# Building weight sums in DRAM: transfers in threes behind a copy that reads the weights loaded two jobs ahead

## The chip, the cores and the metric

The kernel runs on one core of a Trainium2 chip. The metric is device time in microseconds (us). Below, PE is the tensor engine, ACT the scalar engine, DVE the vector engine, POOL the GpSimd engine and SP the sync engine, which only issues DMAs. POOL issues DMAs too, and on POOL every DMA of this program takes engine time for writing its descriptors. All DMAs run on the same 16 DMA engines.

## The reference

One decoder layer on 512 positions of width 1024, in float32:

```
h = rmsnorm(x);  proj = h @ w_in                       # w_in: 1024 x 9232
y_a = short_conv_branch(bg, cg, xv) @ w_a_out
y_b = gated_delta_rule(q, k, v, z, a, b) @ w_b_out
x = x + (sigmoid(ga) * y_a + sigmoid(gb) * y_b) @ w_o  # w_o: 1024 x 1024
h = rmsnorm(x)
x = x + (silu(gate) * val) @ w_down                    # gate, val = causal conv of h @ w_up; w_down: 2816 x 1024
out = rmsnorm(x)
```

## The kernel before

**Products.** Every float32 operand is split into a high part (`wh`, made by ACT) and a low part (`wl`, made by DVE as the raw block minus `wh`; lines 140 and 141), and each product is three matmuls. Some products use a Strassen form with 7 instead of 8 block products.

**Jobs.** `run_jobs` goes through one list of jobs. A job is a weight block of 1 MB and a function `use` that emits its matmuls. While job i runs on PE, block i+1 is split and block i+2 is loaded into one of two `raw` buffers; SP issues the load as soon as the buffer's last reader is through. A plain job (`col_job`) is 48 matmuls of 512 columns. A sum job (`sum_job` with a `SumBlock`) is 84 matmuls of 256 columns, seven products of twelve; its block is split into seven pairs instead of four, and DVE first forms sums of the block's quarters in place (line 161, four additions). In a sum job the third and last product share the half bank `A[:, L]` and its neighbour: after the third product ACT and DVE take it out into `u` (lines 282 and 283), and the seventh product, the last twelve matmuls, must wait for that.

**Engines are in order.** On DVE the splits of the next block stand in one row with the `u` of the job that runs. So a `wl` that waits holds back a `u` behind it.

**Sums in DRAM.** For `w_o` and `w_down` the Strassen sums of the weights are not made by DVE but by DMAs from DRAM to DRAM, some of which accumulate: `Sums.form` (line 1028) issues them on POOL's queue, 256 KB each, 8 for each of 14 row pairs, 112 in all (32 for `w_o`, then 80 for `w_down`). Their generator stands in the queue `adds`. Before the change it is stepped once every four matmuls' worth of columns (`tick`, line 94, every 2048 columns), and it yields twice after each DMA. That paces the program text only: the DMAs stand in POOL's queue in program order, and no DMA waits for PE, so POOL issues them as fast as it gets through them. `adds` is filled in `open_conv` (line 1069), that is with the first of 24 jobs: twelve for the short convolution (C_CG, C_XV, C_BG), four C_GA, four `w_a_out`, four `w_b_out`. After them come 7 jobs for `w_o`, 22 for `w_up` (gate and value in turn; the gates of groups 2 to 9 are sum jobs) and then those for `w_down`. The `w_o` and `w_down` blocks are read from the sums (`raw<-ov`, `raw<-dv`).

**Other work of POOL there.** Four tiny powers in `fin1` (line 1301, the norm before the FFN) and four in `fin2` (line 1543, the last norm).

Of the kernel before, what the change touches and what calls it, by code (L numbers as in the profile page):

```python
# [9 lines left out]
F32 = mybir.dt.float32  # L10
# [19 lines left out]
Y_F = (5, 4, 6, 3)  # L30
WARM = 3
WQ = 12
Y_M = 10


# [24 lines left out]
def layer_kernel(ctx, tc, x, norm_mix_g, w_in, w_ab, conv_a_w, gdn_conv_w, gdn_A_log, gdn_dt_bias,  # L60
# [3 lines left out]
    pe, act, dve, pool = nc.tensor, nc.scalar, nc.vector, nc.gpsimd  # L64
# [5 lines left out]
    const = ctx.enter_context(tc.tile_pool(name="const", bufs=1))  # L70
# [4 lines left out]
    def nm(s):  # L75
        cnt[0] += 1
        return f"{s}{cnt[0]}"
# [5 lines left out]
    chains, mids, backs, evacs, splits, sums_of, adds = (deque() for _ in range(7))  # L83
    nmm = [0]

    def advance(queue, n):
        while n and queue:
            queue[0].step()
            if queue[0].done:
                queue.popleft()  # L90
            else:
                n -= 1

    def tick():
        advance(backs, 1)
        advance(mids, 1)
        advance(chains, 1)
        advance(evacs, 2)
        advance(splits, 1)
        advance(sums_of, 1)  # L100
        advance(adds, 1)

    def drain(queue):
        while queue:
            advance(queue, 1)

    def mm(o, a, b, start, stop, free=False):
        pe.matmul(o, lhsT=a, rhs=b, start=start, stop=stop, skip_group_check=free)  # L108
        nmm[0] += o.shape[-1]
        if nmm[0] >= SLAB * S:  # L110
            nmm[0] -= SLAB * S
            tick()
# [12 lines left out]
    class Block:  # L125
        def __init__(self, src, quarter=(4, P)):
            self.src, self.quarter = src, quarter
            self.raw, self.ready, self.lead = None, False, 2
            self.wh, self.wl = {}, {}

        def load(self):
# [5 lines left out]
        def part(self, name, src):  # L137
            wh = self.wh[name] = wp.tile([P, *self.quarter], F32R, tag="wh", bufs=WQ, name=nm("wh"))
            wl = self.wl[name] = wp.tile([P, *self.quarter], F32R, tag="wl", bufs=WQ, name=nm("wl"))
            act.copy(out=wh, in_=src)  # L140
            dve.tensor_tensor(out=wl, in0=src, in1=wh.bitcast(F32), op=ALU.subtract)  # L141
# [42 lines left out]
    class FormBlock(Block):  # L184
        def __init__(self, runs, names, lead, place):
            super().__init__(None, (S,))
            self.runs, self.names, self.lead, self.place = runs, names, lead, place

        def load(self):
            if self.raw is not None:  # L190
# [13 lines left out]
    def run_jobs(jobs):  # L204
        jobs[1][0].load()
        for i, (block, use) in enumerate(jobs):
            Task(block.split()).finish()
            drain(splits)
            if i + 1 < len(jobs):
                splits.append(Task(jobs[i + 1][0].split()))  # L210
            for j, (later, _) in enumerate(jobs[i + 2:i + 5]):
                if later.lead >= j + 2:
                    later.load()
            use(block.wh, block.wl)


    def piece(w, j, k):
# [7 lines left out]
    def col_job(w, i, xs, consume, pre=None):  # L225
        def use(wh, wl):
            if pre:
                pre()
            x_ = xs() if callable(xs) else xs
            for j in range(GW // P):  # L230
                o = bank()
                products(o, wh, wl, j, x_)
                evacs.append(Task(consume(j, o)))
        return Block(lambda: w[i]), use
# [25 lines left out]
    def sum_job(w, i, xs, sums, consume, place, pre=None):  # L260
        def use(wh, wl):
# [9 lines left out]
            def times(o, form, b, first):  # L271
                mm3(o, [(wh[form][:, k], wl[form][:, k], b[0][:, k], b[1][:, k]) for k in range(ND // 2)],
                    first, not first)
# [50 lines left out]
    def conv(dst, src, wcol, taps):  # L324
        act.activation(out=dst, in_=src, func=AF.Copy, scale=wcol(taps - 1))  # L325
        for j in range(taps - 2, -1, -1):
            sh = taps - 1 - j
            dve.scalar_tensor_tensor(out=dst[:, sh:], in0=src[:, :S - sh], scalar=wcol(j),  # L328
                                     in1=dst[:, sh:], op0=ALU.mult, op1=ALU.add)
            yield  # L330
# [86 lines left out]
    with tc.tile_pool(name="st1", bufs=1) as st1:  # L417
# [79 lines left out]
        def round_k(q):  # L497
            wh = k_block.wh[q] = wp.tile([P, 4, P], F32R, tag="wh", bufs=WQ, name=nm("wh"))
            act.copy(out=wh, in_=k_block.raw[:, q])

        def rest_k(q):
            wl = k_block.wl[q] = wp.tile([P, 4, P], F32R, tag="wl", bufs=WQ, name=nm("wl"))
            dve.tensor_tensor(out=wl, in0=k_block.raw[:, q], in1=k_block.wh[q].bitcast(F32), op=ALU.subtract)
# [267 lines left out]
    def mid(pr, U, um, T, rest):  # L771
        for _ in range(Y_T if pr else Y_T + Y_M):
            yield
# [211 lines left out]
    jobs = []  # L985
# [29 lines left out]
    class Sums:  # L1015
# [12 lines left out]
        def form(self):  # L1028
            steps = [[(V1, W12, False), (V3, W12, False)], [(V1, W11, True), (V3, W22, True)],
                     [(V2, None, False)], [(V2, W22, True)], [(V4, None, False)], [(V4, W21, True)]]  # L1030
            for step in steps:
                for g in self.pairs:
                    for to, q, add in step:
                        src = self.q[g][:, q] if q is not None else self.at(g, V1 if to == V2 else V2)
                        kw = dict(accum_op=ALU.add) if add else {}
                        tc.keep_in_program_order(pool.dma_start(out=self.at(g, to), in_=src, **kw))  # L1036
                        yield
                        yield

# [341 lines left out]
    def ffn(m):  # L1383
        if m < NA:
            return st["aT"][0][:, m, :]
        if len(st["aT"]) == 1:
            st["aT"].append(st["up"].tile([P, NF - NA, S], F32, tag="late", name="aTb"))
        return st["aT"][1][:, m - NA, :]

    def gate_c(g):  # L1390
        def c(j, o):
            m = 2 * g + j
            t = st["cvp"].tile([P, S], F32, tag="g", bufs=4, name=nm("g"))
            yield from conv(t, o, ff_w(m), 3)
            act.activation(out=t, in_=t, func=AF.Silu)
            gates[m] = t
            yield
        return c

    def val_c(g):  # L1400
        def c(j, o):
            m = 2 * g + j
            t = st["cvp"].tile([P, S], F32, tag="v", bufs=2, name=nm("v"))
            yield from conv(t, o, ff_w(NF + m), 3)
            dve.tensor_tensor(out=ffn(m), in0=t, in1=gates.pop(m), op=ALU.mult)
            yield
        return c
# [22 lines left out]
    for g in range(NF // 2):  # L1430
        def up_job(i, c, plain, pre=None):
            if plain:
                return col_job(w_up, i, lambda: st["h2"], c, pre)
            return sum_job(w_up, i, lambda: st["h2"], hsums, c, pair_out)

        last = g == NF // 2 - 1
        gj = up_job(g, gate_c(g), g < 2 or last, (lambda: splits.append(prep_d(prep_a, 0))) if last else None)
        vj = up_job(NF // 2 + g, val_c(g), True)
        jobs += [(gj[0], first_gate), (vj[0], first_val)] if g == 0 else [gj, vj]


# [13 lines left out]
    def prep_d(prep, c):  # L1455
        return Task(prep(ffn_pairs(down_w.pairs[2 * c], 2), xs(), 2 * c % 4))
# [107 lines left out]
    down.append((down_w.low(), use_l))  # L1564
    jobs += [(FormBlock(*what, 2 if i < 2 else min(4, i), down_place(i)), use) for i, (what, use) in enumerate(down)]
    run_jobs(jobs)
    drain(chains)

# [51 lines left out]
```

## Time and profile before

| | us |
|---|---|
| median of three runs | 971.42 (970.35 to 973.03) |
| the profiled execution | 968.61 |
| its span, first to last instruction | 966.90 |
| PE busy in the span | 954.4 |
| DVE busy | 743.9 |
| ACT busy | 506.3 |
| POOL busy | 137.1 |

The profile is of one execution. Busy time of POOL holds the writing of descriptors for its DMAs. A row of the timeline is start in us, length in us, engine, line, what it writes and reads, how many were merged, and in brackets the idle time before and what ended it. PE's matmuls overlap, so their rate is read from the distance of their starts: those of 256 columns start every 0.12 us. "SPq" is a DMA issued by SP; the time to landing is from issue until the data are there.

### The profile page before, as it was taken

To read this page: it belongs to the slowest core of one execution; us is meant where nothing else is said; L and a number is where in the kernel's file an instruction comes from. 1 tells how busy PE (TensorE), PEld (TensorE's weight loads), DVE (VectorE), ACT (ScalarE), POOL (GpSimd) and SP (SyncE) were. 2 spreads that over 40 slices of the span, in tenths; PEclk is the share of its full clock that TensorE was granted. 3 is DMA by queue.
4 is the path that set the end of the run, shared out by engine and by line. 5 is a ranking of instruction groups with operands and counts; after the bars stand their busy time and mean duration, and the time that the engine had idled before them with its cause. 6 is when DMAs were issued, how large, how long until landed. Compare 5 with 4: busy or idle time off the path is not lost. (4 is left out here: it accounts for less than half of the span.)

```text
span 966.9 us, 16043 instructions
## 1 busy us (share of the span) xinstructions
PE 954.4 (99%) x6166; PEld 826.9 (86%) x6166; DVE 743.9 (77%) x1397; ACT 506.3 (52%) x1071; POOL 137.1 (14%) x213
## 2 busy tenths in 40 slices
PE   8999999999999999999999999999999999999996
PEld 6888887987878889899988888998889999888885
DVE  6868686896635968799773479999988888969785
ACT  7795556575444434344651235645645455546463
POOL 3330300202002334234320000100000000000000
PEclk9999999999999999999999999999999999999999
DMA  6443312222222989999995235432232323177342
GB/s 226 156 138 115 100 53 88 74 75 75 55 86 76 226 228 252 252 200 260 275 260 150 87 107 220 164 119 88 88 131 87 129 90 132 44 253 235 99 132 87
DMA packets 51628, 138.10 MB, mean 143 GB/s; under 512 B 21691, under 2 KB 22112, under 8 KB 42848
## 3 DMA queue, kind: packets, MB, share of 16 engines
q1 hardware_dynamic: 39008, 107.72, 32.5%
q0 software_dynamic: 12544, 29.37, 14.8%
q8 instruction: 48, 0.79, 0.3%
q14 instruction: 28, 0.23, 0.1%
HBM read 133.64 MB, written 32.78 MB: 172 GB/s over the span
## 5 line engine op out<-in xcount | busy, mean ns | idle before, releaser
L108 PE MATMUL ps<-hT,wh 128*128 128x512 f32 (+1 forms) x1104 | 318.6, 368 | 1.2 <-DVE u L283 0.8
L140 ACT CAST wh<-raw 128x512 fp32r<-128x512 f32 x350 | 203.6, 618 | 214.3 <-PE ps L108 141.0
L141 DVE TENSOR_TENSOR wl<-raw,wh 128x512 fp32r<-128x512 f32 x350 | 232.3, 688 | 62.4 <-ACT wh L140 60.2
L108 PEld LDWEIGHTS ps<-hT,wh 128*128 128x128 f32 x1104 | 196.9, 189 | 30.1 <-DVE u L283 1.0
L108 PE MATMUL ps<-hT,wl 128*128 128x512 f32 (+1 forms) x552 | 195.2, 362 | 0.0
L108 PE MATMUL ps<-h,wh 128*128 128x512 f32 (+1 forms) x704 | 177.9, 341 | 0.3 <-DVE h L1317 0.3
L108 PEld LDWEIGHTS ps<-h,wh 128*128 128x128 f32 x704 | 122.4, 189 | 15.5 <-DVE h L1317 0.5
L108 PEld LDWEIGHTS ps<-hT,wl 128*128 128x128 f32 x552 | 104.4, 189 | 13.8
L108 PE MATMUL ps<-h,wl 128*128 128x512 f32 (+1 forms) x352 | 114.7, 341 | 0.0
L108 PE MATMUL ps<-wh,xs 128*128 128x512 f32 x312 | 96.2, 389 | 0.0
L108 PEld LDWEIGHTS ps<-h,wl 128*128 128x128 f32 x352 | 66.7, 190 | 7.6
L108 PEld LDWEIGHTS ps<-wh,xs 128*128 128x128 f32 x312 | 58.6, 188 | 12.1
L108 PE MATMUL ps<-wl,xs 128*128 128x512 f32 x156 | 60.7, 389 | 0.0
L108 PE MATMUL ps<-ts,wh 128*128 128x256 f32 x320 | 59.2, 283 | 0.0
L328 DVE SCALAR_TENSOR_TENSOR cv<-ps,wA,cv 128x511 f32<-128x511 f32 (+2 forms) x72 | 53.2, 741 | 4.0 <-ACT cv L325 3.8
L140 ACT CAST wh<-raws 128x512 fp32r<-128x512 f32 x66 | 39.2, 619 | 26.2 <-PE ps L108 12.1
L141 DVE TENSOR_TENSOR wl<-raws,wh 128x512 fp32r<-128x512 f32 x66 | 42.8, 685 | 12.1 <-ACT wh L140 12.1
L108 PEld LDWEIGHTS ps<-ts,wh 128*128 128x128 f32 x320 | 50.6, 192 | 0.0
L1543 POOL TENSOR_TENSOR r<-r,nhalf 128x1 f32<-128x1 f32 x4 | 2.2, 540 | 338.2 <-PE ps L108 331.2
L161 DVE TENSOR_TENSOR raw<-raw 128x512 f32<-128x512 f32 x72 | 49.4, 686 | 0.9
L108 PE MATMUL ps<-us,wh 128*128 128x256 f32 x256 | 47.4, 283 | 0.0
L1036 POOL DMA_DIRECT2D dv<-in_w_down_dram x50 | 35.4, 712 | 58.9 <-issue 58.4
(309 smaller groups left out, 1549.8 us busy)
## 6 DMA issues: line engine op xcount, KB each, us to landing
raw<-in_w_in_dram SPq DMA_DIRECT2D x35, 1024.0 KB, 5.5
raw<-in_w_up_dram SPq DMA_DIRECT2D x22, 1024.0 KB, 4.9
dv<-in_w_down_dram POOLq DMA_DIRECT2D x50, 256.0 KB, 7.8
raws<-dv SPq DMA_DIRECT2D x8, 768.0 KB, 7.0
ov<-in_w_o_dram POOLq DMA_DIRECT2D x20, 256.0 KB, 7.1
raws<-in_w_down_dram SPq DMA_DIRECT2D x10, 512.0 KB, 5.1
raw<-in_w_a_out_dram SPq DMA_DIRECT2D x4, 1024.0 KB, 7.7
raw<-in_w_b_out_dram SPq DMA_DIRECT2D x4, 1024.0 KB, 8.5
```

The source lines that it names most:

```text
L108: pe.matmul(o, lhsT=a, rhs=b, start=start, stop=stop, skip_group_check=free)
L140: act.copy(out=wh, in_=src)
L141: dve.tensor_tensor(out=wl, in0=src, in1=wh.bitcast(F32), op=ALU.subtract)
L161: dve.tensor_tensor(out=r[q], in0=a, in1=b, op=op)
L328: dve.scalar_tensor_tensor(out=dst[:, sh:], in0=src[:, :S - sh], scalar=wcol(j), in1=dst[:, sh:], op0=ALU.mult, op1=ALU.add)
L1036: tc.keep_in_program_order(pool.dma_start(out=self.at(g, to), in_=src, **kw))
L1543: pool.tensor_tensor(out=r, in0=r, in1=nhalf[:, 0:1], op=ALU.pow)
```

## The change

The step of `adds` is taken out of `tick`, and the second `yield` out of `form`. In its place `run_jobs` calls `feed` once for a job whose block of two jobs later is an ordinary 1 MB block (`fed`), as long as there are DMAs left: POOL copies one element of that block's raw buffer, out of its second quarter, into a tile `gate`, and then three DMAs are put out. Blocks read from the sums themselves (`FormBlock`) and the two blocks of the first `w_up` group are not `fed`. Line numbers after the change are 9 or 10 higher (1036 becomes 1046, 1301 becomes 1310).

```
 def tick():
     ...
     advance(sums_of, 1)
-    advance(adds, 1)
 ...
 class Block:
-            self.raw, self.ready, self.lead = None, False, 2
+            self.raw, self.ready, self.lead, self.fed = None, False, 2, True
 ...                                   # FormBlock: fed = False
 def run_jobs(jobs):
             ...
+            if adds and i + 2 < len(jobs) and jobs[i + 2][0].fed:
+                feed(jobs[i + 2][0].raw)
             use(block.wh, block.wl)
+
+    gate = const.tile([1, 1], F32, name="gate")
+
+    def feed(raw):
+        el = raw[0:1, 1].rearrange("p k n -> p (k n)") if len(raw.shape) == 4 else raw[0:1, 1]
+        tc.keep_in_program_order(pool.tensor_copy(out=gate, in_=el[:, 0:1]))
+        advance(adds, FEED)                                   # FEED = 3
 ...
     def form(self):                   # of Sums
                     tc.keep_in_program_order(pool.dma_start(out=self.at(g, to), in_=src, **kw))
                     yield
-                    yield
 ...
+        gj[0].fed = vj[0].fed = g > 0  # the w_up jobs of group g
```

The order of instructions on PE, ACT, DVE and SP is the same as before. On POOL it changes from the place where the sums begin. Before, behind the last power of the delta rule (`fac`), `ov` being the sums of `w_o`:

```order
L911 TENSOR_TENSOR fac_3791<-fac_3791,nhalf 128x8
L1036 DMA ov_388<-in_w_o_dram 128x512 x2
L1036 DMA ov_389<-in_w_o_dram 128x512 x2
L1036 DMA ov_390<-in_w_o_dram 128x512 x2
L1036 DMA ov_391<-in_w_o_dram 128x512 x2
```

and after, where `gate` is the new tile and each `raw` is the buffer of another block of `w_in`:

```order
L921 TENSOR_TENSOR fac_3792<-fac_3792,nhalf 128x8
L223 COPY gate<-raw_3990 1x1
L1046 DMA ov_389<-in_w_o_dram 128x512 x2
L1046 DMA ov_390<-in_w_o_dram 128x512
L223 COPY gate<-raw_4076 1x1
L1046 DMA ov_390<-in_w_o_dram 128x512
L1046 DMA ov_391<-in_w_o_dram 128x512 x2
```

Before, nothing stood between the transfers; now a copy that can only run once a load has landed stands ahead of every three. At the norm before the FFN, before, the last transfers of `w_down` (`dl`) stood ahead of the powers of `fin1`:

```order
L1036 DMA df_386<-in_w_down_dram 128x512
L1036 DMA dl<-in_w_down_dram 128x512 x4
L1301 TENSOR_TENSOR r_6694<-r_6694,nhalf 128x1
L1301 TENSOR_TENSOR r_6721<-r_6721,nhalf 128x1
L1301 TENSOR_TENSOR r_6822<-r_6822,nhalf 128x1
L1301 TENSOR_TENSOR r_6857<-r_6857,nhalf 128x1
```

and after, 63 transfers stand ahead of them and 49, behind 17 copies, follow in the FFN's first half (`raw_6836` is the first gate block of `w_up` that is fed):

```order
L1046 DMA dv_377<-in_w_down_dram 128x512
L1310 TENSOR_TENSOR r_6667<-r_6667,nhalf 128x1
L1310 TENSOR_TENSOR r_6694<-r_6694,nhalf 128x1
L1310 TENSOR_TENSOR r_6795<-r_6795,nhalf 128x1
L1310 TENSOR_TENSOR r_6830<-r_6830,nhalf 128x1
L223 COPY gate<-raw_6836 1x1
L1046 DMA dv_377<-in_w_down_dram 128x512
L1046 DMA dv_378<-in_w_down_dram 128x512 x2
```

So 49 of the 112 transfers have moved from ahead of the norm to behind it. On DVE the order stays, but in 17 of the 18 sum blocks that are fed (all but the first; nine ahead of the norm, eight in `w_up`) the first addition in place now also waits for POOL, which reads the same buffer in its copy. One such block in `w_up` before, with what each row waits for:

```order
L141 TENSOR_TENSOR wl_8570<-raw_8430,wh_8569 128x512 [waits Activation_49]
L1405 TENSOR_TENSOR aTa<-v_8442,g_8357 128x512 [waits DVE_49]
L161 TENSOR_TENSOR raw_8430<-raw_8430 128x512 [waits DVE_49]
L283 TENSOR_TENSOR u_8436<-ps_8432,u_8436 128x256 [waits Activation_49]
L161 TENSOR_TENSOR raw_8430<-raw_8430 128x512 [waits DVE_49] x2
```

and after:

```order
L141 TENSOR_TENSOR wl_8607<-raw_8459,wh_8606 128x512 [waits Activation_49]
L1414 TENSOR_TENSOR aTa<-v_8475,g_8386 128x512 [waits DVE_49]
L161 TENSOR_TENSOR raw_8459<-raw_8459 128x512 [waits DVE_49,Pool_49]
L293 TENSOR_TENSOR u_8469<-ps_8465,u_8469 128x256 [waits Activation_49]
L161 TENSOR_TENSOR raw_8459<-raw_8459 128x512 [waits DVE_49] x2
```

No row has moved; the wait for POOL stands directly ahead of the `u` that PE's last product waits for. In the same way SP's load into a buffer that was copied from now waits for that copy.

## Rows read from the trace of the kernel before

**Rows 1.** Busy times of engines in stretches (from:to and length in us).

```profile
core 0: us, PE busy (x) PEld busy (x) DVE busy (x) ACT busy (x) POOL busy (x), PEclk, DMA share, GB/s
350.00:475.00 125.00, 124.25 (x931) 119.44 (x930) 102.86 (x173) 52.84 (x102) 46.74 (x70) 1.00 0.96 243
650.00:850.00 200.00, 200.00 (x1200) 179.32 (x1199) 179.18 (x279) 104.54 (x182) 0.00 (x0) 1.00 0.27 95
...
682.00:703.00 21.00, 21.00 (x134) 19.11 (x133) 19.68 (x34) 11.31 (x21) 0.00 (x0) 1.00 0.33 116
```

**Rows 2.** What PE waited for from 300 to 960 us (total, times, longest).

```profile
PE ps L108 <- DVE u L283: 0.8, 1, 0.8
PE ps L108 <- DVE h L1317: 0.3, 1, 0.3
```

**Rows 3.** Timeline around PE's one wait in the first half's sum jobs.

```profile
381.52 0.33 SPq L135 DMA_DIRECT2D raw<-in_w_in_dram  x1
...
390.77 1.14 ACT L140 CAST wh<-raw 128x512 fp32r<-128x512 f32 x2 [4.47 <-DMA raw<-in_w_in_dram]
...
391.42 1.29 DVE L141 TENSOR_TENSOR wl<-raw,wh 128x512 fp32r<-128x512 f32 x2 [4.30 <-ACT wh L140]
394.81 0.42 DVE L283 TENSOR_TENSOR u<-ps,u 128x256 f32<-128x256 f32 x1
...
393.89 0.64 PE L108 MATMUL ps<-hT,wh 128*128 128x256 f32 x4
395.28 0.39 PE L108 MATMUL ps<-hT,wh 128*128 128x256 f32 x1 [0.76 <-DVE u L283]
```

**Rows 4.** Landing of SP's weight loads, from 300 to 520 us and from 640 to 850.

```profile
DMA to landing us min/median/max: 7.3/8.4/9.2
...
DMA to landing us min/median/max: 4.8/4.9/5.0
```

**Rows 5.** Transfers of line 1036 on POOL: duration min/median/max, first and last start.

```profile
L1036 POOL DMA_DIRECT2D ov<-in_w_o_dram x20: 523/810/1286, 308.3 to 348.4; - x20
...
L1036 POOL DMA_DIRECT2D dl<-in_w_down_dram x4: 807/820/835, 505.6 to 513.1; - x4
```

**Rows 6.** Timeline of one sum job in `w_up`: SP, ACT, DVE and PE.

```profile
762.80 0.33 SPq L135 DMA_DIRECT2D raw<-in_w_up_dram  x1
769.49 0.33 SPq L135 DMA_DIRECT2D raw<-in_w_up_dram  x1
783.78 0.33 SPq L135 DMA_DIRECT2D raw<-in_w_up_dram  x1
...
769.23 0.61 ACT L140 CAST wh<-raw 128x512 fp32r<-128x512 f32 x1
...
772.50 0.68 DVE L161 TENSOR_TENSOR raw<-raw 128x512 f32<-128x512 f32 x1
773.29 0.42 DVE L283 TENSOR_TENSOR u<-ps,u 128x256 f32<-128x256 f32 x1
...
776.53 0.76 PE L108 MATMUL ps<-h,wh 128*128 128x256 f32 x5
```

**Rows 7.** DVE's `wl` (line 141) from 300 to 520 us and from 640 to 850.

```profile
L141 DVE TENSOR_TENSOR wl<-raw,wh 128x512 fp32r<-128x512 f32 x112 | 72.4, 685 | 15.9 <-ACT wh L140 15.2
...
L141 DVE TENSOR_TENSOR wl<-raw,wh 128x512 fp32r<-128x512 f32 x105 | 69.7, 684 | 17.8 <-ACT wh L140 16.5 <-PE ps L108 1.1
```

**Rows 8.** A small POOL copy, and a `wl` on DVE beside a POOL operation.

```profile
L406 POOL COPY mask<-mfull x4: 200/202/208, 19.8 to 20.5; 32x32 f32<-32x32 f32 x4
...
108.14 1.87 POOL L725 TENSOR_TENSOR um<-U,mask 32x256 f32<-32x256 f32 x2
...
109.32 1.23 DVE L141 TENSOR_TENSOR wl<-raw,wh 128x512 fp32r<-128x512 f32 x1
```

**Rows 9.** First loads of blocks that are read from the sums.

```profile
534.83 0.33 SPq L194 DMA_DIRECT2D raw<-ov  x1
...
816.49 0.33 SPq L194 DMA_DIRECT2D raw<-dv  x1
```

More of the change, by code (lines that the diff above doesn't have):

```diff
@@ L32 @@
 WQ = 12
+FEED = 3
 Y_M = 10
@@ L186, in __init__ @@
             super().__init__(None, (S,))
-            self.runs, self.names, self.lead, self.place = runs, names, lead, place
+            self.runs, self.names, self.lead, self.place, self.fed = runs, names, lead, place, False
         def load(self):
```

## The prediction

> **What bounds the kernel now.** I read the busy times by stretch first, then what PE waited for, then the one wait that has to do with weights, then how long loads and transfers take.
>
> PE is the bound, and it is full. In the stretch in which the sums in DRAM are now built, 350 to 475 us, PE is busy 124.25 of 125 us, though the DMA engines are busy 0.96 of the time; from 650 to 850 us, where half of the transfers will go, it is busy 200.00 of 200, with the DMA engines at 0.27 [rows 1]. From 300 us to the end PE waited twice: 0.8 us for DVE's `u` and 0.3 us in the norm before the FFN [rows 2]. Only the first can have to do with the sums. So the DMA contention is plainly there, and almost none of it reaches PE.
>
> The one wait, in its order [rows 3]: a load is issued at 381.52 and ACT stands 4.47 us for its landing, until 390.77; DVE stands 4.30 us for ACT's `wh`; `u` of the running sum job is behind those splits on DVE and ends at 394.81 + 0.42 = 395.23; PE's last product starts at 395.28. Before it, four matmuls start at 393.89 and every 0.12 us after, so the next was due at 393.89 + 4 x 0.12 = 394.37. PE lost 395.28 - 394.37 = 0.91 us.
>
> **Why that load was late.** Loads land 7.3 to 9.2 us after issue while the transfers run, and 4.8 to 5.0 us where none do [rows 4]. This one took at least 390.77 - 381.52 = 9.25 us, so about 4.3 us longer than alone. POOL's first transfer starts at 308.3 and the last at 513.1 [rows 5]: 204.8 us for 112, or 1.83 us each, back to back, at the pace that the DMA engines and the rings allow. That is the traffic which the change thins out.
>
> **The change part by part.**
>
> *Transfers in threes.* A triple follows the landing of a load, and the next load comes a job later. At the saturated pace a triple takes at most 3 x 1.83 = 5.5 us. In `w_up` two jobs take 783.78 - 762.80 = 21.0 us [rows 6], so a triple has 10.5 us on average, and the DMA engines are no longer full. Ahead of the norm a load will land in something between 4.9 us (alone) and 9.2 us (saturated); since a triple starts only when the load before has landed, I take it nearer to the lower end, 5 to 6 us. The wait of 0.91 us vanishes if its load takes less than 9.25 - 0.91 = 8.3 us. Term: -0.91 us. The bounds are 0 (the load stays as late) and -0.91; there is no other wait of PE on weights to win.
>
> *The transfers moved into the FFN.* 49 transfers go into a stretch that was free of them, where they can only cost. There PE waits for a late block by the same way as in rows 3, so I work out the room there [rows 6]. Load A of a sum block is issued at 762.80 and lands 4.9 us later, at 767.7; its first cast starts at 769.23, 1.5 us after. The running job's `u` ends at 773.29 + 0.42 = 773.71. PE's last product starts with the fifth of the matmuls that begin at 776.53, at 776.53 + 4 x 0.12 = 777.01, so `u` has 3.3 us. A sum block may land 1.5 + 3.3 = 4.8 us later than now, 9.7 us after issue, before PE waits. The latest load of the saturated stretch is 9.25 us. The next load, B, at 769.49, is issued 1.8 us after A landed, so it does run beside A's triple: in the worst case it takes 9.2 us and lands at 778.7; it is a plain block, which PE takes up only after a whole job more. B's triple then runs to 778.7 + 5.5 = 784.2, and load C, the next sum block, issued at 783.78, meets its last 0.4 us. So C, the kind with the least room, is nearly undisturbed. Term: 0, with 4.8 us of cover against 0.4 us expected and 4.3 us at the worst.
>
> *POOL's copies and DVE's new wait.* 38 copies are added. A copy of 32 x 32 elements on POOL takes 0.20 us [rows 8]; one element will take no more. A copy is ready at the landing unless POOL still issues the triple before. DVE's first addition in place, which now waits for it, starts at 772.50, 4.8 us after the landing, and directly behind it stands `u` [rows 6]. Loads are at least 769.49 - 762.80 = 6.7 us apart and a triple takes 5.5 us at the most, so POOL is through; the copy comes some 4.5 us before it is wanted. Queued behind the copy on POOL are its three transfers, and the powers of `fin1` stand behind transfers of a load long landed. SP's next load into the buffer waits for the copy too, but it already waits for the split, which ends later. Term: 0; without the cover it is the slow rival below.
>
> *POOL beside DVE.* Writing descriptors does not slow DVE: `wl` takes 685 ns beside the transfers and 684 ns without [rows 7]. Term: 0.
>
> *Deadlines.* The sums of `w_o` are 32 transfers, done with the eleventh copy, which hangs on a load some ten jobs ahead of the first use at 534.83; those of `w_down` are done with the 38th copy, which hangs on the load of the last sum gate, issued at 783.78, landed by 793, so by some 799 us against a first use at 816.49, and what is left last (`dl`) is used in the last job of all [rows 6, 9]. Term: 0.
>
> *The sum.* 968.61 - 0.91 = 967.70 us against the profiled execution. That execution is 2.81 us below the median of 971.42, which I carry over unchanged: 970.5 us, 0.09% less. A measurement of this kernel tells about 0.3%, 2.9 us, from no change, so this counts as the same.
>
> **The rivals.**
>
> *Late sum blocks in `w_up`* (slower). If the triples make each of the eight sum blocks there land more than 4.8 us later than now, each costs PE what rows 3 show, 0.91 us: 8 x 0.91 = 7.3, so 970.5 + 7.3 = 977.8 us. For it: B's triple and load C do touch, DVE is busy 19.68 of 21 us in the fullest pair of jobs [rows 1] and so recovers slowly, and the new wait on POOL stands just ahead of `u`. Against it: under full saturation loads are late by 4.3 us, and that is still less than 4.8.
>
> *The timed runs hold more of these waits than the profiled one* (faster). The three runs lie 1.7 to 4.4 us above the profiled execution. If what they lose lies in contention that varies from run to run, the change takes that too: 967.7 us for the median. For it: in the saturated stretch loads vary by 1.9 us [rows 4] and the wait of 0.91 us was a matter of one load. Against it: nothing in the trace places the 2.81 us there; they can as well lie outside the span.
>
> *DVE held by the copies* (slightly slower). Beside POOL's operation of 108.14 a `wl` took 1.23 us instead of 0.68 [rows 8]: something there held DVE for 0.55 us. By a copy of 0.2 us twice in 21 us DVE would go from 19.68 to at most 20.1, still below 21, and PE would see nothing. If a copy takes as long as each of the two operations from 108.14, 0.94 us, two of them bring the fullest pair of jobs to 21.6 of 21 us: 0.6 us late there, 971.1 us. The Trainium skill, page "SBUF — State Buffer", section "SBUF: two separate sides", states that DVE with two SBUF inputs and a POOL operation that reads SBUF lock each other out for a whole instruction; that speaks against a copy on POOL, and row 109.32 agrees with it. By that rule the price is a copy's whole length, which is the case just worked out.
>
> **How the numbers follow.** Forecast, one wait gone and nothing lost: 0.74, at 970.5 us, and with the scatter of the three runs (-1.1 and +1.6) 969.4 to 972.1. DVE held: 0.04, at 971.1. Faster, contention in the timed runs: 0.13, at 967.7. Slower, late sum blocks: 0.09, at 977.8. Faster by over 0.3% is below 968.5, slower above 974.3. So faster 0.13, same 0.74 + 0.04 = 0.78, slower 0.09. The range takes in the forecast, the held DVE with the scatter above it, and the faster case, and leaves out the slow one: 967.3 to 973.5 us.
>
> **What would show it.** In the profile after: no wait of PE for `u` near 395 us; loads that land in 5 to 6 us from 340 to 530 us instead of 8.4; POOL's transfers in threes from about 345 to 800 us, the DMA share near 0.6 in both stretches instead of 0.96 and 0.27; no wait of PE between 650 and 850 us. In `w_up`, plain blocks landing later than 4.9 us and sum blocks at about 4.9. I am wrong if PE waits for `u` in the sum jobs of `w_up` (the slow rival; then look whether DVE's first addition stands there waiting for POOL or for ACT), or if the median falls by 3 us with no wait of PE to account for it.

## The result, and the profile after

The changed kernel takes 972.85 us (median of 18 runs, 970.89 to 974.67) against 970.99 us for the kernel before (18 runs, 968.70 to 973.03): ratio 1.002, 95% interval 1.0012 to 1.0029. That is 1.9 us slower where I had forecast 0.9 us faster. It is less than the 0.3% that I had set as the bound, but the interval lies wholly on the other side. The profiled execution took 973.09 us, its span 971.4. Of all executions on record three took 1351 us or more (one of the kernel before, one each of two experiments), and every median and ratio from here on leaves them out.

Nearly all that I had named as signs of the change is there. Lines that stood at 1036, 108 and 135 of the kernel before are 1046, 108 and 135 now; the copy is line 223, `u` line 293. The waits of PE from 300 us to the end (line, releaser: us, times, longest), which answer [rows 2], have lost the one for `u`:

```profile
PE ps L108 <- DVE h L1326: 0.2, 1, 0.2
```

The busy times of the same stretches as in [rows 1] (us of the stretch, PE, PEld, DVE, ACT and POOL with their counts, PE's granted clock, DMA share, GB/s) have PE full in both, and DMA shares of 0.67 and 0.55 where 0.96 and 0.27 stood:

```profile
350.00:475.00 125.00, 125.00 (x938) 120.02 (x937) 103.32 (x174) 54.77 (x105) 28.63 (x45) 1.00 0.67 171
650.00:850.00 200.00, 200.00 (x1203) 179.20 (x1202) 180.24 (x281) 105.07 (x183) 31.56 (x54) 1.00 0.55 150
```

The landings of SP's weight loads, from 300 to 520 us and from 640 to 850, answer [rows 4]:

```profile
DMA to landing us min/median/max: 4.7/4.9/7.0
...
DMA to landing us min/median/max: 4.9/5.7/7.3
```

The copies and the first and the last kind of transfers on POOL (duration in ns min/median/max, first and last start) answer [rows 5]; the transfers now last until 792.7 us instead of 513.1:

```profile
L223 POOL COPY gate<-raw x38: 173/378/1886, 319.3 to 792.2; 1x1 f32<-1x1 f32 x38
...
L1046 POOL DMA_DIRECT2D ov<-in_w_o_dram x20: 523/843/1474, 320.6 to 406.6; - x20
...
L1046 POOL DMA_DIRECT2D dl<-in_w_down_dram x4: 822/830/835, 778.8 to 792.7; - x4
```

One sum job of `w_up` in the timeline answers [rows 6]:

```profile
712.27 0.42 DVE L293 TENSOR_TENSOR u<-ps,u 128x256 f32<-128x256 f32 x1
...
715.46 0.76 PE L108 MATMUL ps<-h,wh 128*128 128x256 f32 x5
```

In that sum job `u` ends at 712.69 and PE's last product starts at 715.46 + 4 x 0.12 = 715.94: 3.25 us of room, as the 3.3 before. PE stood still nowhere for the change. So the lost time has to be in work that PE does. It shows where I had not looked, in the matmuls themselves. Here are PE's matmuls of five kinds, by the tiles that they read: count, duration in ns min/median/max, first and last start in us. Of the two tiles that are named the first is the moving operand (`rhs` of the call) and the second the stationary one (`lhsT`); the rows have those with `wh`, the third that reads `wl` is counted apart. Below, cadence is the time from the start of a matmul to the start of the next. First the kernel before:

```profile
L108 PE MATMUL ps<-ts,wh x320: 283/283/284, 356.1 to 475.3; 128*128 128x256 f32 x160
L108 PE MATMUL ps<-yas,wh x128: 389/389/390, 489.2 to 532.5; 128*128 128x512 f32 x128
L108 PE MATMUL ps<-yb,wh x128: 389/389/390, 532.7 to 576.0; 128*128 128x512 f32 x128
L108 PE MATMUL ps<-us,wh x256: 283/283/284, 664.9 to 817.4; 128*128 128x256 f32 x128
L108 PE MATMUL ps<-wh,xs x312: 388/389/390, 853.1 to 958.9; 128*128 128x512 f32 x156
```

And the same rows of the changed kernel:

```profile
L108 PE MATMUL ps<-ts,wh x320: 277/281/285, 358.2 to 475.5; 128*128 128x256 f32 x160
L108 PE MATMUL ps<-yas,wh x128: 395/395/397, 489.4 to 534.0; 128*128 128x512 f32 x128
L108 PE MATMUL ps<-yb,wh x128: 389/389/396, 534.2 to 577.5; 128*128 128x512 f32 x128
L108 PE MATMUL ps<-us,wh x256: 277/281/285, 667.1 to 818.8; 128*128 128x256 f32 x128
L108 PE MATMUL ps<-wh,xs x312: 388/394/397, 854.5 to 963.4; 128*128 128x512 f32 x156
```

The products of `xs` (in `w_down`, where the change issues nothing) run from 853.1 to 958.9 before, 105.8 us, and from 854.5 to 963.4 after, 108.9 us. Those of `yas` go from 43.3 to 44.6 us; those of `yb`, with the same shape, stay at 43.3. Those of `us` go from 152.5 to 151.7, and `ts` from 119.2 to 117.3, of which 0.9 is the wait. The instructions, their shapes and their order on PE are the same in both kernels, and the granted clock in these stretches is 1.00 (2.4 GHz) in both.

What does differ is where the tiles lie. The change makes a new tile, `gate`, in the pool of constants, which is allocated ahead of most others. It holds 4 bytes and takes 32 per partition, so the tiles of the left side of SBUF (`wh`, `wl`, `hT`, `yb`, `h`), whose pools are laid out from the low end, lie 32 bytes higher; `wh` begins at byte 19200 of a partition where it began at 19168. The pools of the right side (`ts`, `us`, `yas`, `mix`, `xs`) grow from the other end and stay, `ts` at 135136. These places come from the allocation of the program; the traces hold no addresses. The pairs whose cadence changed by more than half a nanosecond are exactly those with one operand on each side.

### The profile page after: what moved, and what is told of

The parts are those of the page before. It is cut to its first block, busy times and chain, and to the rows that moved or that the text cites. A ratio compares the mean times of both kernels' runs of the same rounds, so it can differ in the third digit from the quotient of the medians.

```text
span 971.4 us, 16140 instructions
## 1 busy us (share of the span) xinstructions
PE 958.7 (99%) x6166; PEld 826.1 (85%) x6166; DVE 744.0 (77%) x1397; ACT 506.7 (52%) x1071; POOL 153.4 (16%) x251
## 4 chain that ended last, share of the span: by engine, by line
PE 91%; DVE 3%; ACT 1%; issue 1%; POOL 1%; POOLq 0%
PE ps L108 83%; PE ps L681 1%; PE ps L716 1%; DVE wl L141 1%; PE ps L890 1%; PE ps L910 1%; DVE h L1326 0%; PE ps L899 0%; DVE hn L1312 0%; PE ps L878 0%; PE ps L877 0%; PE ps L854 0%; PE ps L848 0%; POOL r L1310 0%; PE ps L792 0%
## 5 line engine op out<-in xcount | busy, mean ns | idle before, releaser
L108 PE MATMUL ps<-wh,xs 128*128 128x512 f32 x312 | 98.2, 395 | 0.0
L223 POOL COPY gate<-raw 1x1 f32<-1x1 f32 x38 | 16.9, 446 | 279.9 <-DMA raw<-in_w_in_dram 119.3
L108 PE MATMUL ps<-yas,wh 128*128 128x512 f32 x128 | 40.4, 395 | 0.0
```

Source lines behind the costliest of these rows:

```text
L223: tc.keep_in_program_order(pool.tensor_copy(out=gate, in_=el[:, 0:1]))
```

## The experiments

Theory A is that this 32-byte shift of tiles against each other costs the time and that the feed by itself gains what I had forecast. The rivals: the feed costs the time (B), or the slower matmuls are chance of an execution (C). Kernels of one group ran on the same chip beside the kernel before; its median was 971.12 us for the first four, 970.34 for the next four, 971.21 for the last four. Beside the medians I use the traces: the lateness of the same matmul (counted in PE's order, 6166 in all) against the first trace of before, at number 1025 (at 153 us there) and at the last one. The difference between these two leaves the start of the execution out. For the changed kernel it is 4.52 - 2.07 = +2.45 us.

### The shift without the change

```diff
+    spare = const.tile([1, 1], F32, name="spare")
+    nc.gpsimd.memset(spare, 0.0)
```

> The kernel before, with one unused tile of 1x1 in the pool of constants (and one memset of it at the start): nothing of the change, but all tiles of the left side of SBUF lie 32 bytes per partition higher, as they do in the changed kernel. Theory A (the place of the tiles): by the records of the changed kernel the 512-column matmuls whose operands lie on different sides (yas, mix, xs with wh or wl) went from 226.7 to 232-234 ns, some 790 of them, +5.2 us; the 256-column ones of ts and us with wh and wl went from 120.0 to 118.3 ns, 864 of them, -1.5 us; so this kernel is 3.7 us slower than before, 974.7, and shows these four cadences though none of its transfers moved. Theory B (the feed itself costs the time: the POOL copies, the moved transfers): no pair changes, 971.0. Theory C (the slower cadence is chance of an execution): 971.0 in the median, and the cadences of before or after by chance.

It took 973.09 us (12 runs), ratio 1.0029, interval 1.0015 to 1.0043: slower than before, without any of the change. The four cadences came as theory A has them (233.5 ns for `xs`, 118.2 for `ts`), and the trace falls behind by 4.91 - 0.68 = +4.2 us after number 1025. The one surprise is why it is that much: PE's waits, as in [rows 2], show that the old wait for `u` grew:

```profile
PE ps L110 <- DVE u L285: 1.5, 1, 1.5
```

The larger part of that is the load. ACT's row for it (392.01 us) and the issue at 382.19 give 9.8 us to landing, where [rows 3] have 9.25:

```profile
392.01 1.14 ACT L142 CAST wh<-raw 128x512 fp32r<-128x512 f32 x2 [5.14 <-DMA raw<-in_w_in_dram]
```

From the start that was due without the wait to the actual one PE loses 1.68 us here and 0.91 before. Of the 0.77 more, the later landing is 0.57; only 0.2 is PE coming to it sooner, because `ts` runs faster.

### The other side moved instead

```diff
+    side = ctx.enter_context(tc.tile_pool(name="side", bufs=1, side="right"))
+    spare = side.tile([1, 1], F32, name="spare")
+    nc.gpsimd.memset(spare, 0.0)
```

> The kernel before, with the unused 1x1 tile on the right side of SBUF: now yas, mix, xs, ts and us move by 32 bytes and wh, wl, hT, yb stay. Theory A in the form that the distance between the two operands counts: as with the left side moved, 974.7, xs with wh at 233, ts with wh at 118 ns. Theory A in the form that the place of wh and wl alone counts: 971.0 and all cadences of before. Theories B and C: 971.0.

973.82 us (12 runs), ratio 1.0032, interval 1.0018 to 1.0047; cadences 233.3 (`xs`), 118.2 (`ts`), 234.1 (`yas` with `wh`), as in the kernel with the left side moved. The wait for `u` is 1.9 us, behind a load that took 10.2. Neither the place of `wh` nor that of `xs` counts, but the distance between the two.

### The change without its tile

```diff
-    gate = const.tile([1, 1], F32, name="gate")
-        tc.keep_in_program_order(pool.tensor_copy(out=gate, in_=el[:, 0:1]))
+        tc.keep_in_program_order(pool.tensor_copy(out=nhalf[0:1, 7:8], in_=el[:, 0:1]))
```

> The change without its tile: the gating copy writes into a corner of nhalf that nothing reads any more, so no tile moves. Theory A: the whole change but without the 3.7 us, 972.85 - 3.7 = 969.1, i.e. 1.9 us faster than before; cadence of xs with wh 226.7 ns, of ts with wh 120.0 ns; no wait of TensorE for u near 395 us. Theory B: the same as the changed kernel, 972.9. Theory C: 972.9 or less by chance.

969.48 us (11 runs), ratio 0.9981, interval 0.9970 to 0.9992: faster than before, and 3.4 us below the changed kernel, where theory A has 3.7. In the trace it moves by 1.41 - 2.35 = -0.94 us, all of it at the place where the wait for `u` stood, and nothing is lost or won anywhere else. This is what my sum said, -0.91. The rows of `us` and `xs` show that the cadences of before are back:

```profile
L108 PE MATMUL ps<-us,wh x256: 283/283/284, 666.3 to 818.8; 128*128 128x256 f32 x128
L108 PE MATMUL ps<-wh,xs x312: 388/389/390, 854.5 to 960.3; 128*128 128x512 f32 x156
```

Both kernels begin `xs` at 854.5; this one begins its last at 960.3, the changed one at 963.4. B and C fall.

### A tile of 64 bytes

```diff
-    gate = const.tile([1, 1], F32, name="gate")
+    gate = const.tile([1, 16], F32, name="gate")
```

> The change with a gate tile of 64 bytes instead of 4 (which takes 32): the left side lies 64 bytes higher than before. Theory A in the form that only the offset within 64 bytes counts: as without the tile, 969.1, xs with wh at 226.7 ns. Theory A in the form that any move against the right side counts: 972.9, xs with wh at 233 ns. Theory B: 972.9.

965.25 us (median of 4), ratio 0.9938, interval 0.9921 to 0.9955. Neither form of theory A had this: `ts` and `us` did not go back to 120.0 ns but down to 113.9, `xs` to 229, `yas` to 233. So the offset within 64 bytes is not the rule, nor is any move as good as another; the distance counts on a scale of more than 64 bytes. The row of `us`, from 662.8 to 812.8, is 150.0 us long where it was 152.5:

```profile
L108 PE MATMUL ps<-us,wh x256: 276/276/286, 662.8 to 812.8; 128*128 128x256 f32 x128
```

### Other distances

The next four are the change without its tile, with the right side lower by 128 or 192 bytes (`[1, 32]` or `[1, 48]` in the first edit), or with 64 or 32 bytes of room (`[1, 16]` or `[1, 8]` in the second) between `wh`, `wl` and the rest of the left side.

```diff
         st["ya"] = sc.tile([P, ND, S], F32, name="ya")
+        nc.gpsimd.memset(sc.tile([1, 32], F32, name="spare"), 0.0)
...
         xf = up.tile([P, ND, S], F32, tag="late", name="xf2")
+        nc.gpsimd.memset(up.tile([1, 32], F32, name="spare2"), 0.0)
```

> The change without its tile (as in e2_noshift), and the tiles of the right side (ts, us, yas, mix, xs) 128 bytes per partition lower, by a spare tile behind them in their two pools. Seen so far, moving operand's place minus stationary operand's place, taken modulo 256 bytes: at 0 the 256-column matmuls come every 120.0 ns and the 512-column ones every 226.7; at -32 ts and us 118.2, yas 234; at -64 ts and us 113.9, yas 233; xs and mix, whose moving operand is wh, at +32 233.5 and at +64 229. If the pattern repeats every 128 bytes: the same as e2_noshift, 969.5, with 120.0 and 226.7. If it repeats every 256: ts and us at 114 or less, 5 us or more gained on 864 matmuls, and 226.7 or more for the 790 others, so 964 to 969. If the size of the move is no matter, only that there is one: 118 and 233, 973.

> As e5_right128, with 192 bytes, which is +64 modulo 256 for ts, us and yas and -64 for xs and mix: the distance of e3_shift64 with its sign turned. If the sign doesn't count: as e3_shift64, ts and us 113.9, xs 229, yas 233, 965.3. If it is moving minus stationary that counts: yas goes from 233 to 229 and xs and mix from 229 to 233, +4 x 600 ns = 2.4 us, 967.7. If the pattern repeats every 128 bytes it is -64 again for all and the same as e3_shift64 but for the sign of xs.

```diff
     wp = ctx.enter_context(tc.tile_pool(name="wp", bufs=2))
+    gap = ctx.enter_context(tc.tile_pool(name="gap", bufs=1))
+    spare = gap.tile([1, 16], F32, name="spare")
+    nc.gpsimd.memset(spare, 0.0)
```

> The change without its tile, and 64 bytes left free between the pool of the weights (wh, wl) and that of hT, yb, x and h, so that these move against wh and wl, both on the left side; ts, us, yas, mix and xs stay. If the distance between the two operands counts and the side doesn't: hT and h with wh and wl go as ts, us and yas did, 904 matmuls of 256 columns from 119.8 to 114 (-5.2 us) and 1666 of 512 columns, with 192 of yb, from 227 to 229 (+3.7 us) or 233 (+11 us): 968 to 975, cadence of yas and xs 226.7. If only operands on different sides collide: nothing moves, 969.5.

> As e7_hT64, with 32 bytes. If the distance counts: 256 columns from 119.8 to 118.2 (904, -1.4 us), 512 columns from 227 to 233 (1858, +11 us): 979. If only operands on different sides collide: 969.5.

They took 971.72 (ratio 1.0012, 0.9996 to 1.0027), 971.85 (1.0013, 1.0000 to 1.0026), 969.98 (0.9998, 0.9983 to 1.0012) and 976.98 us (1.0073, 1.0047 to 1.0099; 5 runs). The distance counts for two operands on the same side just as well: with 32 bytes of room `h` and `yb` go from 227 to 233 ns, with 64 to 229. And the sign counts for the 512 columns: `yas` at +64 comes to 228.7 and `xs` at -64 to 233.2, the values of the kernel with the 64-byte tile with their places exchanged. For the 256 columns I had that wrong: +64 gives 117.8, not 113.9. And for 128 bytes I had expected 114 ns or less under a period of 256, and 964 to 969 us; it was 118.8 ns, and 971.72 us. From start to start of consecutive matmuls in the traces, with "distance" as moving minus stationary operand in bytes modulo 256:

| distance | 256 columns, ns | 512 columns, ns |
|---|---|---|
| 0 | 120.0 (`ts`, `us`) | 226.1 to 227.3 (`xs`, `yas`, `yb`, `h`) |
| +32 | 117.0 to 117.8 (`h`) | 232.4 to 233.8 (`xs`, `h`, `yb`) |
| -32 | 118.2 to 118.6 (`ts`, `us`) | 231.7 to 234.1 (`yas`) |
| +64 | 117.0 to 118.1 (`h`, `ts`, `us`) | 228.6 to 229.6 (`xs`, `h`, `yb`, `yas`) |
| -64 | 113.8 to 114.1 (`ts`, `us`) | 233.2 to 233.5 (`xs`, `yas`) |
| 128 | 118.6 to 119.1 (`ts`, `us`) | 231.1 to 237.5 (`xs`, `yas`) |

Each value is the mean for one tile with `wh` or with `wl`. The values in a row come from different tiles, and mostly from different kernels, and they agree within 1.5 ns but for `yas` at -32 and 128. There the matmuls with `wl` differ from those with `wh`; over both, `yas` comes to 233.3 at -32 and at 128, as all others of 512 columns at +32 and -64 do (`xs` at 128: 232.4). A period of 128 bytes is out. One of 256 fits: the distances of before are, by the allocation, whole multiples of 256, odd ones for `ts` (453) and even ones for `hT` (192), and 192 bytes the one way did what 64 the other way did.

### Each pair at its best distance

For 512 columns the best seen is 0, for 256 columns -64. Only `ts` and `us` have to move:

```diff
-        st["ts"] = [sc.tile([P, 4, 4, HS], F32R, tag=f"t{i}", name=f"ts{i}") for i in range(2)]
+        st["ts"] = [sc.tile([P, 16 * HS + 64], F32R, tag=f"t{i}", name=f"ts{i}")[:, 48:48 + 16 * HS]
+                    .rearrange("p (a b c) -> p a b c", a=4, b=4) for i in range(2)]
```

and the same for `us`, once on the change without its tile and once on the kernel before.

> The change without its tile (as in e2_noshift), and only ts and us set 64 bytes (modulo 256) below wh and wl, by 192 bytes of room in front of them in their own buffers; yas, mix, xs, hT and h stay at distance 0. If the distance of the two operands sets the cadence of each pair by itself: ts and us 113.9 ns as in e3_shift64 and all others as in e2_noshift (120.0, 226.7), 864 x 6.1 ns = 5.3 us less than e2_noshift's 969.5: 964.2, 6.5 us under before. If e3_shift64's gain came from something else that it moved: 969.5, or between.

> The kernel before, with the same edit of ts and us and nothing of the feed. The products of the sum jobs take 5.3 us less if the distance sets them: 966 if all of it counts. But the wait for u near 395 us grows by what TensorE arrives earlier there (0.5 to 1 us of the 5.3 are gained before it), and further sum jobs could come to wait for late blocks: 966.5 to 968, with the wait at 1.4 to 2 us in place of 0.9. If the feed were worth nothing beyond its 1.0 us: 966; e9_ts_apart then lies 1 us under this one, otherwise 2 us or more.

The first took 962.50 us (4 runs), ratio 0.9909, interval 0.9895 to 0.9924: 8.7 us faster than the kernel before and 10.4 below the changed one, the best of this study. In the trace it gains 5.70 + 1.00 = 6.7 us, 0.94 of it by the feed and 5.8 by the products of `ts` and `us`; I had 5.3. Their rows, with `xs` as before:

```profile
L108 PE MATMUL ps<-ts,wh x320: 276/276/286, 357.2 to 472.2; 128*128 128x256 f32 x160
L108 PE MATMUL ps<-us,wh x256: 276/276/286, 661.8 to 811.7; 128*128 128x256 f32 x128
L108 PE MATMUL ps<-wh,xs x312: 388/389/389, 847.4 to 953.2; 128*128 128x512 f32 x156
```

The second took 965.16 us (6 runs), ratio 0.9947, interval 0.9925 to 0.9969. I had 966.5 to 968. It gains 5.2 us in the trace, and its wait for `u` is longer than that of before, though not the 1.4 to 2 us that I had, since the load landed after 8.9 us this time:

```profile
PE ps L108 <- DVE u L283: 1.1, 1, 1.1
```

So the feed is worth 6.7 - 5.2 = 1.5 us once the products are faster. The medians are 2.7 us apart, with few runs and a wide interval on the second; more than 1.5 is not shown.

### The threes without the copy

```diff
     def feed(raw):
-        el = raw[0:1, 1].rearrange("p k n -> p (k n)") if len(raw.shape) == 4 else raw[0:1, 1]
-        tc.keep_in_program_order(pool.tensor_copy(out=nhalf[0:1, 7:8], in_=el[:, 0:1]))
         advance(adds, FEED)
```

> The change without its tile and without the copies: the transfers go in threes at the same places of POOL's stream, but nothing makes them wait for the block of two jobs later. If handing them out per job is what helps: no wait for u near 395 us, 969.5 as e2_noshift. If the copy's wait is what keeps the batch out of the way of the block's load: loads land later than the 4.7 to 7.0 us of the change (7 to 9 as before), and the wait at 395 us is back in part, 0.3 to 0.9 us: 969.8 to 970.5.

977.58 us (4 runs), ratio 1.0069, interval 1.0044 to 1.0095: 8 us worse than with the copies, far more than either theory had. The order in the program alone holds POOL back at one place, the powers of the norm `fin1`, where it waits for DVE. From 622 us it issues all that is left in one row. The loads of `w_up` then run beside full DMA engines. PE's waits from 300 us on:

```profile
PE ps L108 <- DVE u L290: 6.2, 3, 4.7
```

Two stretches of 20 us, in the columns of [rows 1]:

```profile
680.00:700.00 20.00, 15.28 (x102) 14.26 (x101) 14.57 (x24) 7.21 (x14) 6.62 (x11) 0.91 0.97 279
700.00:720.00 20.00, 20.00 (x113) 17.80 (x113) 14.36 (x24) 10.42 (x19) 5.73 (x7) 0.92 0.89 183
```

And the landings of SP's weight loads from 640 to 850 us, whose longest is 10.3 us in place of 7.3:

```profile
DMA to landing us min/median/max: 4.8/4.9/10.3
```

Of the three waits one is the old one near 395 us (0.8) and two, 5.4 us together, fall between 650 and 760. Behind the first of these, in which PE stands still for 4.7 us, is a late sum block. ACT waited for it:

```profile
695.92 1.14 ACT L140 CAST wh<-raw 128x512 fp32r<-128x512 f32 x2 [8.59 <-DMA raw<-in_w_up_dram]
```

That block's load was issued at 686.16, where before it was at 682.72 with PE only 0.28 us earlier: its buffer came free some 3.2 us later, and then it took 9.7 us. So lateness adds up from block to block. The two stretches have a granted clock of 0.91 and 0.92 where there was 1.00, and all of that is one piece at the lower level, 1.2 GHz, from 696.4 to 703.2 us, which begins while PE stands:

```profile
696.50:703.20 6.70, 4.95 (x18) 4.47 (x19) 6.48 (x12) 3.30 (x8) 2.45 (x3) 0.50 0.86 158
```

By the starts of its matmuls the trace loses 8.2 us from 693 to 723 us: 4.9 and 1.0 at the two waits, and 2.4 in the matmuls between the first wait and 704 us, at the lower clock. This is my slow rival, late sum blocks in `w_up`, and the copy is what keeps it away.

### The kernel before, once more

> The kernel before, unchanged, profiled once more. In the ten traces so far the same matmuls of the first 36 us end 0 to 2.4 us later than in the first trace of before, whatever the kernel. If that is chance of an execution: this trace too starts its later matmuls up to 2.4 us later from the first 36 us on (about 1.5 us in the middle), and the cadences after that are those of before to 0.1 ns: 968.6 to 971. If the start belongs to a kernel's layout: 0.0 us late, 968.6.

969.23 us. Its matmuls are 0.42 us late at number 205 (36 us), 0.76 at 1025, and 0.60 at the end, since its wait for `u` is 0.6 instead of 0.8. So the start of an execution varies with nothing changed, by 0.8 us between these two. Other kernels start up to 2.4 us late, which the two traces of before don't show, and the latest of those starts go with a lower granted clock in the first 25 us. That stretch, in the columns of [rows 1], in the first trace of before:

```profile
0.00:25.00 25.00, 21.71 (x138) 16.69 (x138) 15.77 (x39) 18.01 (x42) 8.62 (x27) 1.00 0.67 226
```

and in the change without its tile:

```profile
0.00:25.00 25.00, 20.30 (x119) 15.91 (x120) 13.66 (x35) 15.67 (x38) 8.63 (x27) 0.93 0.67 219
```

In the second the clock stands at the lower level, 1.2 GHz, once more from 12.4 to 15.8 us:

```profile
12.40:15.80 3.40, 3.40 (x16) 3.14 (x17) 3.40 (x10) 3.40 (x9) 0.00 (x0) 0.50 0.78 233
```

Of fourteen traces seven have 0.93 there, and their number 1025 is 1.4 to 2.4 us late; seven have 1.00 and are 0 to 1.0 us late (2.0 in the one where `hT` itself was slowed by 32 bytes). In the seven with 0.93 the clock first rises between 4.5 and 5.8 us and falls back for 3.4 us; in the other seven it rises between 6.3 and 7.7 us and stays. Kernels with and without the feed, and with and without moved tiles, are in both groups.

## Why the prediction was wrong, point by point

**The late load and its wait.** Right. -0.91 us was forecast, and the wait is gone in the changed kernel; the change without its tile gains 0.94 us in the trace, at that place alone, with an interval of 0.8 to 2.9 us for the medians. Loads land after a median of 4.9 us there, where I had 5 to 6; the longest was 7.0, under the 8.3 that I had asked for.

**The transfers in the FFN.** Right in the sum: no wait, and the room of `u` stays at 3.2 us. Which loads are late I had wrong: the sum block issued at 701.89 took 5.7 us and the one at 785.40 took 6.7, where I had said that sum blocks stay at about 4.9; a plain one at 729.44 took 7.3. Against 4.8 us of cover the 1.8 us more are harmless. The kernel without the copies used the cover up and more. My price for it, 0.91 us for each of eight blocks, was wrong in its shape: two waits of up to 4.7 us, and a lower clock behind them.

**Copies, POOL beside DVE, deadlines.** Right: none of them shows in the change without its tile. A copy takes 0.38 us in the median and 1.89 at the most, where I had 0.20 as the upper bound, from a larger copy at the start of the kernel; POOL has the room. Nor are loads at least 6.7 us apart, as I read from two of them: the trace of before has two at 682.72 and 685.73. `wl` takes 687 ns in both stretches of the changed kernel, against 685 and 684 in [rows 7]: 112 x 2 + 105 x 3 ns, 0.5 us of DVE's time in all, beside 38 copies that together take 16.9 us; the 18 `wl` that a copy runs beside take 686 ns. The Trainium skill, page "SBUF — State Buffer", section "SBUF: two separate sides", has the two engines lock each other out for a whole instruction; in `wl` these rows show none of it, nor do PE's waits. Whether the copies of up to 1.89 us are long because they waited for DVE was not tested.

**The sum.** Here the forecast failed: 968.61 - 0.91 lacks a term. I costed each instruction that the diff adds or moves, and took all others to cost what they did. The diff has one line that is no instruction, `gate = const.tile([1, 1], F32, name="gate")`, and I gave it no term. It is worth the missing 3.4 us: +3.1 for `xs`, +1.3 for `yas`, -0.9 for `ts`, -0.8 for `us` and the rest, +0.7, for the products of `mix`, by the rows above and the same rows of the change without its tile. With the feed's -0.94 that gives +2.5, which is the trace's +2.45; the medians have 1.86, with an interval of 1.2 to 2.8. No rival of mine could have come out there, since all of them were waits. That 972.85 lies inside my range of 967.3 to 973.5 is luck. The upper part of the range was there for a DVE held by the copies, which did not come, and from the held DVE's 971.1 and the scatter of 1.6 I should have written 972.7 as its end.

**Profile and median.** Carrying the 2.81 us over was a little too much for before, whose median over 18 runs was 970.99, 2.4 us above the profiled execution. For the changed kernel the median is 0.2 us below it, so by the profiles alone the change would cost 4.5 us; 2.07 of that is the start of the execution. My fast rival had put it down to contention with the transfers. The traces speak for another place: the profiled execution of before had the earliest start of the fourteen, its repetition was up to 0.8 us later from the start, others up to 2.4. That the timed runs of before lose their 2.8 us there was not traced.

## What to carry to other kernels

A new tile is part of a change, even one of 4 bytes: compare the places of the tiles that PE reads before and after, and if they moved against each other, read the duration of the matmuls by tile in a stretch that the change doesn't touch. Take the shift out (write into space that is free anyway) before judging the rest of a change by a median. In a kernel that PE bounds, the distance between the moving and the stationary operand is a setting worth trying in itself; here it brought 5.8 us, six times what the feed brought.

## What the runs showed that I had not expected

- The cadence of float32 matmuls, with nothing else on the way, depends on the distance between their two operands within a partition: 113.8 to 120.0 ns for 256 columns and 226 to 234 ns, 237 in one case, for 512, at the same granted clock. The best distance differs between the two shapes. What makes it so was not tried; only that the distance decides, and that 256 bytes fits as its period, is shown.
- With the transfers as they were, the wait for `u` varied from 0.6 to 1.9 us, mostly by its load, which landed after 8.9 to 10.2 us. Faster products lengthen such a wait too: in the kernel before with `ts` and `us` at -64 PE was due 0.66 us earlier behind the load's issue, the load landed 0.34 us sooner, and PE's loss grew from 0.91 to 1.23 us.
- During a stand of PE of 4.7 us the granted clock fell to 1.2 GHz for 6.8 us, which cost 2.4 us more.
- The first 25 us have a granted clock of 1.00 or 0.93; with 0.93 the execution was 1.4 to 2.4 us late at matmul 1025. What decides between them stays open.
